# A hybrid decoder block in fp32: small transfers spread between weight loads, and the S5 rotation tables as a task of their own

## The chip, the cores and the metric

The kernel runs on one core of one Trainium2 chip. The core has TensorE (PE: matrix products), VectorE (DVE), ScalarE (ACT), GpSimd (POOL) and SyncE (SP), which here only starts DMA transfers. Each engine works through its own queue of instructions in order and waits on semaphores for the others. The metric is the device time of one execution in microseconds; lower is better. Times of a kernel are the median of several runs.

## The reference

One layer of a decoder block over 256 tokens of width 2048, all in float32:

```python
xn = rms_norm(x, norm_mix_g)
u_s5, u_lru, q, k, v, gate_logits = split(xn @ w_in)      # 2048 -> 1024 + 1024 + 3*1024 + 3*2048
g_s5, g_lru, g_attn = split(sigmoid(gate_logits + b_gate))
merged = (g_s5 * (s5(u_s5) @ w_br_s5) + g_lru * (rglru(u_lru) @ w_br_lru)
          + g_attn * (stick_breaking_attention(q, k, v) @ w_br_attn))
h = x + merged @ w_out
hdn = relu(rms_norm(h, norm_mlp_g) @ w_up)                # 2048 -> 8192
return rms_norm(h + (hdn * hdn) @ w_down, final_norm_g)
```

`s5` is a complex diagonal state space layer (64 groups of 16 channels with 64 states each: `h = lam_bar * h + b_bar u`, then the real part of `c h`, a skip, GELU, and a sigmoid gate over `w_glu`). `rglru` is a convolution of width 4, two block-diagonal gates, and a real linear recurrence. The attention has 8 heads of 128; a weight is `exp(log_sigmoid(z) + sum of log_sigmoid(-z) over the later keys)`, causal.

## The kernel before, in words

**The weight stream.** All dense weights pass in one fixed order as 520 units of 512 KB (128 partitions x 2 x 512 columns): 0 to 15 the LRU inputs, 16 to 31 the S5 inputs, then for each of four column blocks of the LRU gate 8 units of `w_in` and 4 of `w_br_lru` (32 to 79), 80 to 127 six chunks of k, q and v, then four times 8 + 4 for the attention gate and `w_br_attn` (128 to 175), 176 to 231 the S5 gates, `w_glu` and `w_br_s5`, 232 to 263 `w_out`, and then `w_up` and `w_down`. A unit is loaded by SP (L130, `raw`, three buffers), and since a product in float32 is made of three products of shorter floats, ACT rounds it to `hi` (L146) and DVE subtracts to get `lo` (L147; three buffers each). PE uses a unit in `chunk` (24 matmuls of 256 columns, L225 to L227) or in `chunk_tok` and `pair_tok` (12 matmuls of 512 columns, L241 to L243 and L276 to L278): hi times hi, lo times hi, hi times lo. The PE groups in the profile are called `mm_`, `mt_` and `mp_` for these three.

**Side work.** Everything else is written as Python generators with `yield` between their steps. `later(gens, rate)` makes a task of them, and after each unit `pump()` advances each task by `rate` steps. What a step issues is placed behind that unit's matmuls and the casts made with it. There is no other planner: the number of yields and the rate set the order of the side work against the weight units on each engine; the compiler's scheduler then settles the rows of each queue.

**The side work that the change touches.** `s5_params` makes the S5 parameters. `lru_half` runs half of the LRU: convolution, gates, tanh, exp, square root, scan. `s5_scan` (rate 1.27) runs 8 blocks: for each, four `ps_v` products (their inputs are spread over partitions by 12 small transfers, `stk`, L627, on SP), a copy (L653), a rotation by a table of cosine and sine, four scans, and a rotation back. The table of a block, `tc` and `ts` of 128x1024, comes from `s5_tables`: a sum on DVE (L604), a rounding on ACT (L606) and DVE (L607), Abs (L609) and two Sins on ACT (L610, L611). `gates` brings a piece of the gate bias over SP (`gb`, L739), runs a gate chunk on PE, and then a multiply and add on DVE (L744) and a Sigmoid on ACT (L745). `attention` runs each head's logits `z`, `s = ln(1 + exp(-|z|))` (L789 to L792, with DVE at L793 and L794), a cumulative sum on PE (`ps_c`, L800 to L802) and an Exp (L805). ACT's functions come in sets, and a function of another set needs an `ACT_TABLE_LOAD` ahead of it on ACT's queue. The second norm's sum over the columns is one small matmul group `ps_n` (L977). The residual `x_res` (2 MB) is loaded at L918 and the final norm's weights `gfb` (1 MB) at L989, both started from ACT's queue.

Of the kernel before, what the change touches and what calls it, by code (L numbers as in the profile page):

```python
# [9 lines left out]
F32 = mybir.dt.float32  # L10
# [36 lines left out]
def hybrid_block(ctx: ExitStack, tc: tile.TileContext, io, out):  # L47
# [62 lines left out]
    st = {"load": 0, "split": 0, "use": 0}  # L110
# [121 lines left out]
    def chunk_tok(name, c, k, xs, hold=0, done=None):  # L232
# [12 lines left out]
        for g in range(ng - hold):  # L245
# [5 lines left out]
            anchor["pe"] = mm.ins  # L251
            pump()
# [158 lines left out]

    def s5_params():
# [55 lines left out]
        for k, (p, q, op) in enumerate(((cb_, ib_, ALU.add), (ib_, cb_, ALU.subtract))):  # L468
# [5 lines left out]
            for h in range(2):  # L474
                r_ = slice(64 * h, 64 * h + 64)
                nc.vector.tensor_tensor(ce[r_, k, :, h, :], u[r_, 0], u[r_, 1], op)
                yield

# [43 lines left out]

    def lru_half(c, us):
        parts = []
        for m in range(2):
            if m == 0:
                t = [lp.tile([P, 2, L], F32, tag=n_, name=f"lru_{n_}{c}") for n_ in ("xc", "r", "i", "th")]
            else:
                w4 = [pp.tile([P, 2, 2, L], F32, tag=n_, name=f"lru_{n_}{c}", bufs=2) for n_ in ("tc", "ts")]
                t = [w_[:, k] for w_ in w4 for k in range(2)]  # L530
# [8 lines left out]
        yield  # L539
# [12 lines left out]
        yield  # L552
# [42 lines left out]
    def s5_tables(b):  # L595
        c = pp.tile([P, NT, 16, 16], F32, tag="tc", name=f"tc{b}", bufs=2)
        s = pp.tile([P, NT, 16, 16], F32, tag="ts", name=f"ts{b}", bufs=2)
        q = slice(b * NT, (b + 1) * NT)
        sh = [P, NT, 16, 16]
        f = "p n a b -> p (n a b)"  # L600
        cf, sf = c.rearrange(f), s.rearrange(f)

        def gen():
            nc.vector.tensor_tensor(c, fhi[:, q, :].unsqueeze(3).broadcast_to(sh), flo[:, q, :].unsqueeze(2).broadcast_to(sh), ALU.add)  # L604
            yield
            nc.scalar.activation(sf, cf, AF.Identity, bias=magic)  # L606
            nc.vector.scalar_tensor_tensor(sf, sf, -MAGIC, cf, ALU.add, ALU.subtract)  # L607
            yield
            nc.scalar.activation(cf, sf, AF.Abs)  # L609
            nc.scalar.activation(sf, sf, AF.Sin, scale=-TURN)  # L610
            nc.scalar.activation(cf, cf, AF.Sin, scale=-TURN, bias=half_pi)  # L611
            yield
        f = "p n a b -> p n (a b)"
        return (c.rearrange(f), s.rearrange(f)), gen()

# [15 lines left out]
    def s5_scan():  # L631
# [3 lines left out]
        tabs, more = s5_tables(0)  # L635
        yield from more
# [5 lines left out]
        for _ in range(4):  # L642
            yield
        tt = nc.vector.tensor_tensor
        for b in range(WT):
            c, s = tabs
# [9 lines left out]
            more = iter(())  # L656
            if b + 1 < WT:
                s5_split(b + 1)
                tabs, more = s5_tables(b + 1)
                yield  # L660
# [11 lines left out]
            next(more, None)  # L672
# [482 lines left out]
```

## Time and profile before

| | |
|---|---|
| median of three runs | 1522.82 us (1517.03, 1522.82, 1524.22) |
| the profiled execution | 1518.29 us, its span 1516.4 us |
| busy in the span | PE 1489.1 us (98%), DVE 1176.4 (78%), ACT 783.9 (52%), POOL 35.1 (2%) |
| mean granted clock of PE | 0.995 |
| HBM traffic | 282.71 MB read, 188 GB/s over the span |
| weight units on SP's queue | 512 KB each, about 4.2 us from issue to landing |

Busy time counts an instruction from its start to its modelled end. A row of a timeline has the start, the duration, the engine, the line, the operation and its tiles, and in brackets how long the engine had been idle before it and what released it. A row of the waits says which engine waited at which line for which engine's line: the total, how many times, and the longest. `SPq` and `ACTq` are transfers started from those engines' queues.

### The profile page before, as it was taken

The numbers are of one execution on the slowest core, as the hardware profiler recorded it, in microseconds if no ns is written. First come the engines' busy times: TensorE is split into PE (matmuls) and PEld (weight loads), VectorE is DVE, ScalarE is ACT, GpSimd is POOL, SyncE is SP. The second block draws the span as 40 slices with busy tenths as digits, with TensorE's granted clock in tenths as the row PEclk, the third lists the DMA queues.
The fourth block names the chain that finished last, engine by engine and source line by source line (L and its number), as shares of the span: only waits on it lengthen the run. The fifth ranks groups of instructions, "written<-read, shape, count | busy, mean of one in ns | idle before, by whom it ended". The sixth has DMA issues, their size and how long they took to land.

```text
span 1516.4 us, 19895 instructions
## 1 busy us (share of the span) xinstructions
PE 1489.1 (98%) x7518; PEld 1260.0 (83%) x7518; DVE 1176.4 (78%) x1468; ACT 783.9 (52%) x920; POOL 35.1 (2%) x60
## 2 busy tenths in 40 slices
PE   9998999999999999999999999999999999999997
PEld 9996888989887878988787888888888888888886
DVE  6767988897988989689699797568855787558965
ACT  6767556565765564544355444344433444344443
POOL 1400000000000000000000000000000000000011
PEclk9999999999999999999999999999999999999999
DMA  9445766655555756565756556666666666666664
GB/s 291 152 151 180 214 205 201 187 182 170 176 174 179 211 185 210 185 204 187 268 179 189 185 181 207 194 191 198 193 195 192 192 190 198 191 194 192 193 196 152
DMA packets 88914, 292.41 MB, mean 193 GB/s; under 512 B 12786, under 2 KB 17010, under 8 KB 88562
## 3 DMA queue, kind: packets, MB, share of 16 engines
q1 hardware_dynamic: 88386, 287.93, 61.0%
q10 hardware_dynamic: 432, 3.21, 0.6%
q8 instruction: 59, 0.97, 0.3%
q14 instruction: 37, 0.30, 0.1%
HBM read 282.71 MB, written 2.10 MB: 188 GB/s over the span
## 4 chain that ended last, share of the span: by engine, by line
PE 81%; DVE 11%; issue 4%; ACT 2%; DMA 2%; SPq 0%; DVEq 0%; ACTq 0%
PE mt_w_up L242 6%; PE mt_w_up L243 6%; PE mt_w_up L241 6%; PE mt_w_in L242 5%; PE mt_w_in L243 5%; PE mt_w_in L241 5%; DVE lo L147 4%; PE mt_w_down L242 4%; PE mt_w_down L241 4%; PE mt_w_down L243 4%; PE mp_w_down L277 4%; PE mp_w_down L278 4%; PE mp_w_down L276 4%; PE mm_w_in L227 4%; PE mm_w_in L225 4%
## 5 line engine op out<-in xcount | busy, mean ns | idle before, releaser
L146 ACT CAST hi<-raw 128x1024 fp32r<-128x1024 f32 (+1 forms) x521 | 546.4, 1051 | 629.6 <-PE mt_w_up L243 131.6
L147 DVE TENSOR_TENSOR lo<-raw,hi 128x1024 fp32r<-128x1024 f32 (+1 forms) x521 | 638.2, 1226 | 289.4 <-ACT hi L146 285.6
L242 PE MATMUL mt_w_in<-lo,xhi 128*128 128x512 f32 x448 | 176.0, 393 | 3.5 <-DVE lo L147 3.4
L241 PE MATMUL mt_w_in<-hi,xhi 128*128 128x512 f32 x448 | 175.0, 395 | 0.2 <-ACT hi L146 0.2
L243 PE MATMUL mt_w_in<-hi,xlo 128*128 128x512 f32 x448 | 175.1, 391 | 0.0
L241 PE MATMUL mt_w_up<-hi,hhi 128*128 128x512 f32 x448 | 174.3, 389 | 0.0
L242 PE MATMUL mt_w_up<-lo,hhi 128*128 128x512 f32 x448 | 174.3, 389 | 0.0
L243 PE MATMUL mt_w_up<-hi,hlo 128*128 128x512 f32 x448 | 174.3, 389 | 0.0
L227 PE MATMUL mm_w_in<-xhi,lo 128*128 128x256 f32 x512 | 145.4, 286 | 4.7 <-DVE lo L147 4.7
L225 PE MATMUL mm_w_in<-xhi,hi 128*128 128x256 f32 x512 | 146.5, 286 | 0.4 <-ACT hi L146 0.4
L226 PE MATMUL mm_w_in<-xlo,hi 128*128 128x256 f32 x512 | 145.7, 285 | 0.0
L729 DVE STREAM_TRANSPOSE reluT<-relu 32x256 f32<-32x256 f32 x256 | 111.5, 435 | 4.2
L242 PEld LDWEIGHTS mt_w_in<-lo,xhi 128*128 128x128 f32 x448 | 84.6, 189 | 23.2 <-DVE lo L147 6.7
L227 PEld LDWEIGHTS mm_w_in<-xhi,lo 128*128 128x128 f32 x512 | 98.7, 194 | 5.7 <-DVE lo L147 5.7
L242 PE MATMUL mt_w_down<-lo,hd_hi 128*128 128x512 f32 (+1 forms) x272 | 102.5, 377 | 0.0
L241 PE MATMUL mt_w_down<-hi,hd_hi 128*128 128x512 f32 (+1 forms) x272 | 102.4, 377 | 0.0
L243 PE MATMUL mt_w_down<-hi,hd_lo 128*128 128x512 f32 (+1 forms) x272 | 102.4, 376 | 0.0
L277 PE MATMUL mp_w_down<-lo,hd_hi 128*128 128x512 f32 x256 | 99.8, 390 | 0.1
L225 PEld LDWEIGHTS mm_w_in<-xhi,hi 128*128 128x128 f32 x512 | 99.1, 194 | 0.9 <-ACT hi L146 0.7
L276 PE MATMUL mp_w_down<-hi,hd_hi 128*128 128x512 f32 x256 | 99.6, 389 | 0.0
L278 PE MATMUL mp_w_down<-hi,hd_lo 128*128 128x512 f32 x256 | 99.6, 389 | 0.0
L226 PEld LDWEIGHTS mm_w_in<-xlo,hi 128*128 128x128 f32 x512 | 99.2, 194 | 0.1
(299 smaller groups left out, 2356.1 us busy)
## 6 DMA issues: line engine op xcount, KB each, us to landing
raw<-in_w_in SPq DMA_DIRECT2D x175, 512.0 KB, 4.2
raw<-in_w_up SPq DMA_DIRECT2D x128, 512.0 KB, 4.3
raw<-in_w_down SPq DMA_DIRECT2D x128, 512.0 KB, 4.2
raw<-in_w_out SPq DMA_DIRECT2D x32, 512.0 KB, 4.2
raw<-in_w_br_lru SPq DMA_DIRECT2D x16, 512.0 KB, 4.2
raw<-in_w_br_attn SPq DMA_DIRECT2D x16, 512.0 KB, 3.9
raw<-in_w_br_s SPq DMA_DIRECT2D x16, 512.0 KB, 4.2
stk<-ux SPq DMA_DIRECT2D x96, 64.0 KB, 4.0
```

The source lines that it names most:

```text
L146: anchor["act"] = nc.scalar.copy(h[:, k, :], r[:, k, :]).ins
L147: anchor["dve"] = nc.vector.tensor_tensor(l_[:, k, :], r[:, k, :], h[:, k, :].bitcast(F32), ALU.subtract).ins
L225: nc.tensor.matmul(o, wh[:, kk, s], xh, start=first and ct % 2 == 0, stop=False, skip_group_check=True)
L226: nc.tensor.matmul(o, wh[:, kk, s], xl, start=False, stop=False, skip_group_check=True)
L227: mm = nc.tensor.matmul(o, wl[:, kk, s], xh, start=False, stop=last and ct % 2 == 1, skip_group_check=True)
L241: nc.tensor.matmul(banks[j], xh[:, s], wh[:, a:b], start=kt == 0, stop=False)
L242: nc.tensor.matmul(banks[j], xh[:, s], wl[:, a:b], start=False, stop=False)
L243: return nc.tensor.matmul(banks[j], xl[:, s], wh[:, a:b], start=False, stop=kt == ng * UK - 1)
L276: nc.tensor.matmul(o, xh[:, s], wh[:, kk, :], start=kt == 0, stop=False)
L277: nc.tensor.matmul(o, xh[:, s], wl[:, kk, :], start=False, stop=False)
L278: mm = nc.tensor.matmul(o, xl[:, s], wh[:, kk, :], start=False, stop=kt == ng * UK - 1)
L729: nc.vector.transpose(d_[32 * a:32 * a + 32, :, :, 32 * b:32 * b + 32], s_[32 * b:32 * b + 32, :, :, 32 * a:32 * a + 32])
```

## The change

It does seven things. (1) `s5_tables` becomes a task of its own that starts six steps after it is made, with more yields; before its Sins it pauses while a gate chunk is open and fewer than three of its units are left (`st["gate"]`, `st["left"]`). The first table is made at the end of `s5_params`. (2) `lru_half` gives up one yield and puts one into a loop; its second tiles are allocated once. (3) The first block's `stk` transfers get a yield after each `s5_stack`. (4) The gate bias is loaded three steps later. (5) The residual is loaded in four pieces from SP's queue, one in four steps. (6) The final norm's weights are loaded from SP's queue, at a later place of the program. (7) The second norm gets three more yields ahead of `ps_n`.

```diff
--- before.py
+++ after.py
@@ -107,7 +107,7 @@
             "w_out": D, "w_up": D, "w_down": DFF}
 
...
-    st = {"load": 0, "split": 0, "use": 0}
+    st = {"load": 0, "split": 0, "use": 0, "gate": False, "left": 0}
 
     def pieces(i):
         return [slice(k, k + 1) for k in range(UK)] if i == 0 else [slice(0, UK)]
@@ -249,6 +249,7 @@
                 for j in range(len(cols)):
                     mm = mms(j, g * UK + kk, wh[:, kk, :], wl[:, kk, :])
             anchor["pe"] = mm.ins
+            st["left"] = ng - 1 - g
             pump()
         held = [next_unit() for _ in range(hold)]
         for j in range(len(cols)):
@@ -409,6 +410,34 @@
         nc.sync.dma_start(bco, io["s5_b"])
         yield
 
+    def s5_tables(b):
...
+        def gen():
+            nc.vector.tensor_tensor(c, fhi[:, q, :].unsqueeze(3).broadcast_to(sh), flo[:, q, :].unsqueeze(2).broadcast_to(sh), ALU.add)
+            yield
+            yield
+            nc.scalar.activation(sf, cf, AF.Identity, bias=magic)
+            nc.vector.scalar_tensor_tensor(sf, sf, -MAGIC, cf, ALU.add, ALU.subtract)
+            yield
+            yield
+            nc.scalar.activation(cf, sf, AF.Abs)
+            yield
+            while st["gate"] and st["left"] < 3:
+                yield
+            nc.scalar.activation(sf, sf, AF.Sin, scale=-TURN)
+            nc.scalar.activation(cf, cf, AF.Sin, scale=-TURN, bias=half_pi)
+            yield
+        f = "p n a b -> p n (a b)"
+        return (c.rearrange(f), s.rearrange(f)), gen()
+
+    tab0 = []
+
     def s5_params():
         lr, li, dt, a, b, n, w, den, sh, ch, ea, em, xr, xi, cr, ci = (prm[:, k, :] for k in range(16))
         g = nc.gpsimd
@@ -475,6 +504,9 @@
                 r_ = slice(64 * h, 64 * h + 64)
                 nc.vector.tensor_tensor(ce[r_, k, :, h, :], u[r_, 0], u[r_, 1], op)
                 yield
+        tabs, more = s5_tables(0)
+        tab0.append(tabs)
+        yield from more
 
     nq = later([norm1()], 1)
     later([s5_load()], 1)
@@ -520,14 +552,15 @@
     ylru_hi = ypool.tile([P, WT, L], F32R, tag="yhi", name="ylru_hi")
     ylru_lo = ypool.tile([P, WT, L], F32R, tag="ylo", name="ylru_lo")
 
+    lw = [pp.tile([P, 2, 2, L], F32, tag=n_, name=f"lru_{n_}", bufs=2) for n_ in ("tc", "ts")]
+
     def lru_half(c, us):
         parts = []
         for m in range(2):
             if m == 0:
                 t = [lp.tile([P, 2, L], F32, tag=n_, name=f"lru_{n_}{c}") for n_ in ("xc", "r", "i", "th")]
             else:
-                w4 = [pp.tile([P, 2, 2, L], F32, tag=n_, name=f"lru_{n_}{c}", bufs=2) for n_ in ("tc", "ts")]
-                t = [w_[:, k] for w_ in w4 for k in range(2)]
+                t = [w_[:, k] for w_ in lw for k in range(2)]
             cts = [(j, slice(4 * c + 2 * m + j, 4 * c + 2 * m + j + 1)) for j in range(2)]
             parts.append((us[m], cts, *t))
         for u, cts, xc, r, i_, th in parts:
@@ -536,7 +569,6 @@
                 for s in range(1, 4):
                     nc.vector.scalar_tensor_tensor(xc[:, j, s:], u[:, j, :L - s], cw[:, 3 - s, k], xc[:, j, s:], ALU.mult, ALU.add)
                 yield
-        yield
         for u, cts, xc, r, i_, th in parts:
             for j, k in cts:
                 ps = pss.tile([P, CH], F32, tag="ps", name=f"ps_l{c}_{k.start}")
@@ -549,7 +581,7 @@
             for j, k in cts:
                 nc.scalar.activation(th[:, j, :], r[:, j, :], AF.Tanh, scale=sp4[:, k])
             nc.vector.tensor_tensor(i_, i_, xc, ALU.mult)
-        yield
+            yield
         for u, cts, xc, r, i_, th in parts:
             for j, k in cts:
                 nc.scalar.activation(r[:, j, :], r[:, j, :], AF.Exp, scale=nsp8[:, k])
@@ -591,27 +623,6 @@
 
 
     S5_RATE = 1.27
-
...
     def s5_split(ct):
         bx = [ux[:, 2 + i, :].rearrange("p (r g s) -> p r g s", r=2, g=2) for i in range(2)]
@@ -632,17 +643,18 @@
         v = ypool.tile([P, 2, NT, L], F32, tag="yhi", name="s5_v")
         t12 = ypool.tile([P, 2, NT, L], F32, tag="ylo", name="s5_t")
         vr, vi, t1, t2 = v[:, 0], v[:, 1], t12[:, 0], t12[:, 1]
-        tabs, more = s5_tables(0)
-        yield from more
+        tabs = tab0[0]
+        more = None
         s5_split(0)
         yield
         yield
         for t in range(NT):
             s5_stack(t)
-        for _ in range(4):
             yield
         tt = nc.vector.tensor_tensor
         for b in range(WT):
+            if more is not None:
+                finish(more)
             c, s = tabs
             t3 = pp.tile([P, NT, L], F32, tag="t3", name=f"t3_{b}")
             for t in range(NT):
@@ -653,10 +665,10 @@
                 nc.scalar.copy(v[:, :, t, :], v2(ps))
                 if t % 2:
                     yield
-            more = iter(())
             if b + 1 < WT:
                 s5_split(b + 1)
                 tabs, more = s5_tables(b + 1)
+                more = later([chain_of(6, more)], S5_RATE)
                 yield
             tt(t1, vr, c, ALU.mult)
             yield
@@ -669,7 +681,6 @@
             tt(vr, vr, s, ALU.mult)
             yield
             tt(t3, t3, vr, ALU.subtract)
-            next(more, None)
             yield
             for x_ in (t1, t3):
                 for t in range(NT):
@@ -678,11 +689,9 @@
                     if b + 1 < WT and x_ is t1:
                         s5_stack(t)
                     yield
-            next(more, None)
             tt(t2, t1, c, ALU.mult)
             yield
             tt(vr, t3, s, ALU.mult)
-            next(more, None)
             yield
             tt(t2, t2, vr, ALU.subtract)
             yield
@@ -702,6 +711,11 @@
             if b % 2:
                 gq.append(later([gelu(b)], 1.0))
 
+    def chain_of(n, gen):
+        for _ in range(n):
+            yield
+        yield from gen
+
     def tt_scan(o, r, i):
         nc.vector.tensor_tensor_scan(o, r, i, 0.0, ALU.mult, ALU.add)
 
@@ -736,8 +750,17 @@
     def gates(idx, c, alloc):
         gb = tmp.tile([P, CH], F32, tag="gbias", name=f"gb{idx}_{c}", bufs=1)
         o = idx * D + c * CH
-        nc.sync.dma_start(gb, repeat(io["b_gate_row"][:, o:o + CH], P))
+
+        def bias():
+            for _ in range(3):
+                yield
+            nc.sync.dma_start(gb, repeat(io["b_gate_row"][:, o:o + CH], P))
+            yield
+
+        later([bias()], 1.0)
+        st["gate"] = True
         banks = chunk_tok("w_in", GATE0 + 4 * idx + c, D, xs)
+        st["gate"] = False
         gts = []
         for j in range(2):
             g = alloc(c, j).rearrange("p a l -> p (a l)")
@@ -915,7 +938,15 @@
     mlp = ctx.enter_context(tc.tile_pool(name="mlp", bufs=1))
     gp = small("norm_mlp_g")
     x_tok = mlp.tile([P, 2, D], F32, name="xres")
-    nc.scalar.dma_start(x_tok, io["x_res"])
+
+    def x_load():
+        for c in range(4):
+            s = slice(c * CH, (c + 1) * CH)
+            nc.sync.dma_start(x_tok[:, :, s], io["x_res"][:, :, s])
+            for _ in range(4):
+                yield
+
+    later([x_load()], 1.0)
     mf.append(chained(mq, split_tok(3, mlp.tile([P, 4, L], F32, tag="reluT", name="mT3", bufs=2))))
     hT = act.tile([P, KT, L], F32, tag="m16", name="hT")
     hhi = act.tile([P, KT, L], F32R, tag="xhi", name="hhi")
@@ -970,7 +1001,8 @@
             yield
         for n in (2, 1):
             nc.vector.tensor_tensor(hT[:, 0:n, :], hT[:, 0:n, :], hT[:, n:2 * n, :], ALU.add)
-        yield
+        for _ in range(4):
+            yield
         a = hT[:, 0, :]
         ps = pss.tile([P, CH], F32, tag="ps", name="ps_n2")
         for t in range(2):
@@ -986,7 +1018,6 @@
     ho = mlp.tile([P, 2, D], F32, name="ho")
     ssq = mlp.tile([P, 2, 6], F32, name="ssq")
     rf = mlp.tile([P, 2], F32, name="rf")
-    nc.scalar.dma_start(gfb, repeat(io["final_norm_g"], P))
 
     def down_evac(t, s, bank):
         nc.vector.scalar_tensor_tensor(h_tok[:, t, s], bank, rs2[:, t:t + 1], h_tok[:, t, s], ALU.mult, ALU.add)
@@ -1079,6 +1110,8 @@
                         total(t, c)
                     nc.gpsimd.tensor_tensor(ho[:, t, s], h_tok[:, t, s], gfb[:, s], ALU.mult)
 
+        if q == 1:
+            nc.sync.dma_start(gfb, repeat(io["final_norm_g"], P))
         pair_tok("w_down", 0, FQ, hs_, down_done)
         for c in range(2, 4):
             if q == NQ - 1 and c == 3:
```

What the order becomes on SP around the first gate chunk. The rows are transfers in the order in which SP starts them; the first `raw` of `in_w_br_lru` is unit 40. Before:

```order
L130 DMA raw_1484<-in_w_in 128x1024
L627 DMA stk<-ux 32x2x256
L130 DMA raw_1508<-in_w_in 128x1024
L627 DMA stk<-ux 32x512
L627 DMA stk<-ux 32x2x256 x2
L627 DMA stk<-ux 32x512
L627 DMA stk<-ux 32x2x256 x2
L627 DMA stk<-ux 32x512
L627 DMA stk<-ux 32x2x256 x2
L627 DMA stk<-ux 32x512
L627 DMA stk<-ux 32x2x256
L130 DMA raw_1538<-in_w_br_lru 128x1024
```

Now:

```order
L638 DMA stk<-ux 32x512
L638 DMA stk<-ux 32x2x256
L130 DMA raw_1490<-in_w_in 128x1024
L638 DMA stk<-ux 32x512
L638 DMA stk<-ux 32x2x256 x2
L638 DMA stk<-ux 32x512
L638 DMA stk<-ux 32x2x256
L130 DMA raw_1515<-in_w_in 128x1024
L638 DMA stk<-ux 32x2x256
L638 DMA stk<-ux 32x512
L638 DMA stk<-ux 32x2x256
L130 DMA raw_1536<-in_w_br_lru 128x1024
```

The small transfers that stood in one block ahead of unit 40 lie between the loads of the last units of the gate chunk.

On ACT shortly behind a gate chunk. First the second column block of the LRU gate, from the cast of unit 54 on, in the branch chunk behind the gate chunk, before:

```order
L146 CAST hi_1883<-raw_1854 128x1024
L745 ACTIVATE gate_1_0_1873<-gate_1_0_1873 128x512
L745 ACTIVATE gate_1_1_1876<-gate_1_1_1876 128x512
L146 CAST hi_1902<-raw_1881 128x1024
L606 ACTIVATE ts_1660<-tc_1659,magic 128x1024
L146 CAST hi_1923<-raw_1900 128x1024
L609 ACTIVATE tc_1659<-ts_1660 128x1024
```

and now:

```order
L146 CAST hi_1887<-raw_1858 128x1024
L433 ACT_TABLE_LOAD
L433 ACTIVATE ts_1614<-ts_1614 128x1024
L768 ACT_TABLE_LOAD
L768 ACTIVATE gate_1_0_1877<-gate_1_0_1877 128x512
L768 ACTIVATE gate_1_1_1880<-gate_1_1_1880 128x512
L434 ACT_TABLE_LOAD
L434 ACTIVATE tc_1613<-tc_1613,half_pi 128x1024
L146 CAST hi_1908<-raw_1885 128x1024
L146 CAST hi_1927<-raw_1906 128x1024
```

A table's two Sins have come to stand around the gates' Sigmoids, ahead of the cast of unit 55. Then the same place in the attention gate's second column block, from the cast of unit 150 on, before:

```order
L146 CAST hi_4654<-raw_4623 128x1024
L609 ACTIVATE tc_4380<-ts_4381 128x1024
L610 ACT_TABLE_LOAD
L610 ACTIVATE ts_4381<-ts_4381 128x1024
L745 ACT_TABLE_LOAD
L745 ACTIVATE gate_1_0_4644<-gate_1_0_4644 128x512
L745 ACTIVATE gate_1_1_4647<-gate_1_1_4647 128x512
L611 ACT_TABLE_LOAD
L611 ACTIVATE tc_4380<-tc_4380,half_pi 128x1024
L146 CAST hi_4676<-raw_4652 128x1024
L146 CAST hi_4695<-raw_4674 128x1024
```

and now:

```order
L146 CAST hi_4658<-raw_4629 128x1024
L146 CAST hi_4677<-raw_4656 128x1024
L768 ACT_TABLE_LOAD
L768 ACTIVATE gate_1_0_4648<-gate_1_0_4648 128x512
L768 ACTIVATE gate_1_1_4651<-gate_1_1_4651 128x512
L146 CAST hi_4696<-raw_4675 128x1024
L146 CAST hi_4733<-raw_4694 128x1024
```

The table is gone from that place, and the Sigmoids stand behind the cast of unit 151.

On ACT in the second half of the attention, between the casts of units 126 and 129 (`z` and `s` are those of heads 6 and 7, `ts` and `tc` a table). Before:

```order
L146 CAST hi_4044<-raw_4009 128x1024
L789 COPY z_4031<-ps_z_4033 128x384
L790 ACTIVATE s_4032<-z_4031 128x384
L791 ACTIVATE s_4032<-s_4032 128x384
L792 ACTIVATE s_4032<-s_4032 128x384
L146 CAST hi_4088<-raw_4042 128x1024
L789 COPY z_4075<-ps_z_4077 128x384
L790 ACTIVATE s_4076<-z_4075 128x384
L791 ACTIVATE s_4076<-s_4076 128x384
L805 ACTIVATE z_3965<-z_3965 128x384
L792 ACTIVATE s_4076<-s_4076 128x384
L146 CAST hi_4114<-raw_4086 128x1024
```

and now, from head 6's copy on:

```order
L812 COPY z_4041<-ps_z_4043 128x384
L433 ACT_TABLE_LOAD
L433 ACTIVATE ts_3759<-ts_3759 128x1024
L813 ACTIVATE s_4042<-z_4041 128x384
L434 ACTIVATE tc_3758<-tc_3758,half_pi 128x1024
L814 ACT_TABLE_LOAD
L814 ACTIVATE s_4042<-s_4042 128x384
L828 ACTIVATE z_3975<-z_3975 128x384
L815 ACT_TABLE_LOAD
L815 ACTIVATE s_4042<-s_4042 128x384
L812 COPY z_4081<-ps_z_4083 128x384
L146 CAST hi_4094<-raw_4052 128x1024
```

Two Sins of a table now stand among the attention's Abs, Exp and Ln, with loads of function sets between them; a further Exp and Ln of head 7, each with a load ahead, follow behind the casts of units 127 to 129.

More of the change, by code (lines that the diff above doesn't have):

```diff
@@ L410, in s5_load @@
         yield
+    def s5_tables(b):
+        c = pp.tile([P, NT, 16, 16], F32, tag="tc", name=f"tc{b}", bufs=2)
+        s = pp.tile([P, NT, 16, 16], F32, tag="ts", name=f"ts{b}", bufs=2)
+        q = slice(b * NT, (b + 1) * NT)
+        sh = [P, NT, 16, 16]
+        f = "p n a b -> p (n a b)"
+        cf, sf = c.rearrange(f), s.rearrange(f)
+        def gen():
[16 more added lines that the diff above has]
+    tab0 = []
     def s5_params():
@@ L593, in hybrid_block @@
     S5_RATE = 1.27
[L595 to L604, printed above, removed]
-            yield
[L606 to L614, printed above, removed]
     def s5_split(ct):
@@ L972, in norm2 @@
             nc.vector.tensor_tensor(hT[:, 0:n, :], hT[:, 0:n, :], hT[:, n:2 * n, :], ALU.add)
-        yield
+        for _ in range(4):
+            yield
         a = hT[:, 0, :]
```

## The prediction

> **What bounds the kernel now.** I read the busy shares, then what TensorE (PE) waited for, then slices of 40 us, then the timelines around the waits.
>
> ```profile
> span 1516.4 us, 19895 instructions
> PE 1489.1 (98%) x7518; PEld 1260.0 (83%) x7518; DVE 1176.4 (78%) x1468; ACT 783.9 (52%) x920; POOL 35.1 (2%) x60
> ```
> ```profile
> PE mm_w_in L227 <- DVE lo L147: 4.7, 5, 1.9
> PE mt_w_in L242 <- DVE lo L147: 3.4, 5, 1.8
> PE ps_n L977 <- DVE hT L972: 2.3, 1, 2.3
> PE mt_w_br_attn L241 <- ACT hi L146: 2.2, 1, 2.2
> PE mt_w_br_lru L241 <- ACT hi L146: 2.0, 1, 2.0
> PE mp_w_out L277 <- DVE lo L147: 0.8, 1, 0.8
> PE mp_w_out L276 <- ACT hi L146: 0.6, 1, 0.6
> ```
> PE is busy 98% of the span, so a change of side work can give back only what PE waits, plus what a lowered clock costs after a wait. The second fence (total us, times, longest) says where: a weight half (hi from ScalarE, ACT; lo from VectorE, DVE) that comes late because its engine was in side work, and once a norm matmul placed too early. The slices (length, busy us and counts of PE, PEld, DVE, ACT, POOL, then granted clock, DMA share, GB/s) put places to them:
>
> ```profile
> 80.00:120.00 40.00, 37.19 (x262) 35.17 (x261) 28.26 (x42) 28.65 (x42) 0.00 (x0) 0.96 0.46 142
> 120.00:160.00 40.00, 35.89 (x145) 28.26 (x144) 28.39 (x35) 25.05 (x33) 0.00 (x0) 0.91 0.63 197
> 480.00:520.00 40.00, 37.41 (x176) 29.18 (x175) 34.37 (x39) 25.40 (x31) 0.00 (x0) 1.00 0.60 184
> 640.00:680.00 40.00, 40.00 (x178) 33.14 (x177) 32.97 (x45) 17.45 (x18) 0.00 (x0) 1.00 0.65 200
> 720.00:760.00 40.00, 38.59 (x168) 31.07 (x167) 27.83 (x36) 15.52 (x15) 0.00 (x0) 1.00 0.77 264
> 800.00:840.00 40.00, 36.71 (x162) 29.39 (x161) 36.69 (x59) 20.34 (x25) 0.00 (x0) 1.00 0.60 185
> ```
> The slice at 640 is what an undisturbed stretch looks like: 40.00 of 40.00 in 178 matmuls, so a unit of 12 of them takes 2.7. A clock of 0.96 is 0.04 x 40 = 1.6 us lost, one lowering; 0.91 is 3.6 us, two. They follow some waits of about 2 us and not others: none at 480 or 800, where the waits were 2.2 and 2.3. So I price a lowering at 1.7 us and its chance after a wait of 2 us or more at about 0.6 (three of five).
>
> **The change, part by part.** Units count the weight tiles from 0, as in the order of instructions.
>
> *Second LRU half to the first branch (units 25 to 42).* Before:
>
> ```profile
> 91.05 1.22 DVE L147 TENSOR_TENSOR lo<-raw,hi 128x1024 fp32r<-128x1024 f32 x1
> 92.32 0.41 PE L227 MATMUL mm_w_in<-xhi,lo 128*128 128x256 f32 x1 [1.92 <-DVE lo L147]
> 131.71 7.04 SPq L627 DMA_DIRECT2D stk<-ux  x11
> 138.79 1.56 SPq L130 DMA_DIRECT2D raw<-in_w_br_lru  x3
> 135.13 1.28 ACT L745 ACT_TABLE_LOAD   x1
> 141.59 1.31 ACT L745 ACTIVATE gate<-gate 128x512 f32<-128x512 f32 x2 [5.18 <-DVE gate L744]
> 142.81 2.13 ACT L146 CAST hi<-raw 128x1024 fp32r<-128x1024 f32 x2
> ```
> Eleven small stk transfers hold SP's queue for 7.04 us ahead of the first branch weight, and ACT waits 5.18 us for the gate with the cast of that weight behind it: PE stands 2.0 us at unit 40 (mt_w_br_lru). The longest wait of mt_w_in for lo, 1.8, is at unit 36. With smaller ones the slice from 120 lacks 40 - 35.89 = 4.1 us, and 3.6 to the clock: 7.7. Now the stk transfers lie between weights, and the cast of unit 40 stands ahead of the gates; since a gate operation of DVE now stands ahead of lo 40, I leave 1.5 of the 2.0 there. Gain 7.7 - 1.5 = 6.2. Against it, the first table moves here. DVE gets the table's sum, 1.1 to 1.2 like every operation on 1024 columns, ahead of lo 26, and nothing covers it: lo 26 starts straight behind other work and PE already waits 1.92 for it: +1.1. ACT gets two Sins (1.07 and 1.15 in the next fence) and one load more (1.28), 3.5 in all, ahead of the casts of units 31 and 32. A cast may start when the unit three before it is done, which leaves it 2 x 2.7 less its own 1.05, a lead of 4.3; of this the LRU's operations in the same place take most, so 0.9 of waiting at 31 and 0.7 at lo 32. Sum -6.2 + 1.1 + 0.9 + 0.7 = -3.5; carrying each engine's new order by hand through the same durations gives -4.7. **I take -4** (-6 if unit 26 absorbs the sum, -2 if a new wait lowers the clock).
>
> *Gate chunk ends.* Before, at the last one of attention:
>
> ```profile
> 476.76 1.05 ACT L609 ACTIVATE tc<-ts 128x1024 f32<-128x1024 f32 x1
> 477.83 1.28 ACT L610 ACT_TABLE_LOAD   x1
> 479.13 1.07 ACT L610 ACTIVATE ts<-ts 128x1024 f32<-128x1024 f32 x1
> 480.20 1.28 ACT L745 ACT_TABLE_LOAD   x1
> 481.49 1.16 ACT L745 ACTIVATE gate<-gate 128x512 f32<-128x512 f32 x2
> 482.65 1.28 ACT L611 ACT_TABLE_LOAD   x1
> 483.95 1.15 ACT L611 ACTIVATE tc<-tc,half_pi 128x1024 f32<-128x1024 f32 x1
> 485.00 2.93 ACT L146 CAST hi<-raw 128x1024 fp32r<-128x1024 f32 x3
> ```
> The gates fall between the two Sins, so three loads stand in 485.00 - 476.76 = 8.2 us of ACT work ahead of the cast of unit 151; PE waits 2.2 and its slice lacks 2.6. In the new order only one load and the gates are left there: 1.28 + 1.16 = 2.4, behind the cast and less than a unit's 2.7. **-2.8** (-3.5 to -2.2). But the same row of three loads, without the Abs, now stands ahead of the cast of unit 55, the place of unit 151 in the second LRU gate, where before were the gates alone. It is 1.05 shorter, so the wait is 2.2 - 1.05 = 1.1, and some 0.4 at a following unit: **+1.5** (0.5 to 3.8, with a lowering). The pause that the diff adds looks at chunks whose gate is still open; here the task goes on just after.
>
> *Attention, second half.* Before, with s and z of 128x384:
>
> ```profile
> 404.79 0.48 ACT L789 COPY z<-ps_z 128x384 f32<-128x384 f32 x1 [0.49 <-PE ps_z L788]
> 405.30 0.53 ACT L790 ACTIVATE s<-z 128x384 f32<-128x384 f32 x1
> 407.57 0.51 ACT L792 ACTIVATE s<-s 128x384 f32<-128x384 f32 x1
> 407.99 1.03 ACT L146 CAST hi<-raw 128x1024 fp32r<-128x1024 f32 x1
> 408.71 0.42 DVE L794 TENSOR_TENSOR s<-s,keep 128x256 f32<-128x256 f32 x1
> L800 PE MATMUL ps_c<-s,tri x8: 377/379/381, 403.1 to 414.8; 128*128 128x256 f32 x8
> ```
> The last head's s is ready at 409.1 and PE uses it at 414.8: 5.7 us of cover. No load stands between these operations, since one set preloaded at L807 holds Exp and Ln. Now a table's Sins stand among them; behind these Exp and Ln are each given a load of their own. From the copy of head 6 to the last Ln of head 7, ACT gets five loads (6.4), two Sins (2.2) and two casts that were behind (2.1): 10.7 us. Less the 5.7 it is 5.0 of waiting, some 1.3 at unit 127 (its cast is behind the Sins) and 3.7 at the last ps_c; DVE's extra 1.22 ahead of keep is inside what is uncertain. **+5** (2 if heads run earlier, 7 if DVE adds its own), and with 0.6 x 1.7 = 1.0 for a lowering **+6**.
>
> A change of set is priced here by its row, 1.28: the Abs ahead of the load at 477.83 had ended at 477.81, and the Sin started 0.02 behind the load. [...]
>
> *w_out.* Before, the residual x (2 MB, ACT's queue) stands against the weights:
>
> ```profile
> 719.80 0.33 ACTq L918 DMA_DIRECT2D xres<-in_x_res  x1
> 729.08 1.05 ACT L146 CAST hi<-raw 128x1024 fp32r<-128x1024 f32 x1 [6.57 <-DMA raw<-in_w_out]
> 730.38 0.54 ACTq L989 DMA_DIRECT2D gfb<-in_final_norm_g  x1
> xres<-in_x_res ACTq DMA_DIRECT2D x1, 2048.0 KB, 8.6
> ```
> Its 8.6 us make a weight late and PE loses 0.6 + 0.8 = 1.4, the lack of slice 720. In four pieces on SP's queue, three or four weights from first to last, that goes. The 1 MB of gfb now stands on that queue ahead of one weight: by the 2 MB row half of 8.6, 4.3 us, against a cast's lead of about 4 behind it: 0 to 0.8. **-1.2** (-1.6 to 0).
>
> *Second norm.* ps_n goes four steps later, behind more units' matmuls, so that hT is ready: the 2.3 of the third wait goes, and nothing else waits for rs2 before the end of w_down's first group. **-2.3** (-2.5 to -1.5). The gate bias, three steps later, has a gate chunk of 8 units to land: 0.
>
> Sum: -4 - 2.8 + 1.5 + 6 - 1.2 - 2.3 = **-2.8 us**.
>
> **The rivals.** (a) *The table in attention is hidden*: if head 6 and 7 start earlier, since DVE and PE have less ahead of them, the 10.7 us meet 5.7 plus the idle ACT time of the stretch (0.49 and what lies between 408 and 411). Then attention costs 0 to 2: -2.8 - 5 = **-7.8**. For it: ACT is 52% busy. Against: the casts stand in the same queue, in that order.
> (b) *The other side: table switching by one engine.* Place: ACT between units 126 and 130. If head 7's chain runs into the casts of 128 and 129, these hold back their raw buffers and the next weights start late, so the wait goes on: +9 with a sure lowering of 1.7 in place of +6, and unit 55 with one, +3.2 in place of +1.5. Sum -2.8 + 4.7 + 1.7 = **+3.6**. It decides once the lead of casts after 128 falls to zero; by hand about 1.8 us of it is left.
> (c) *The waits only move*: the first table's parts at units 26, 31 and 32 each lower the clock, 3.4, and unit 40 stays at 2: the first part is 0 and the sum **+1**.
> [...]
>
> **How the numbers follow.** Chances: my sum 0.45, (a) 0.25, (b) 0.15, (c) 0.11, (d) 0.04. The profiled execution took 1518.29, its span 1516.4 and 1.9 around it. The median of the three runs shown is 1522.82, between 1517.03 and 1524.22, so the profiled one stands low among them. The sum gives 1515.5 from the profiled execution and 1520.0 from the median; nothing here says which a further run is like, and I take **1517**. Range: (a) from the profiled execution, 1510.5, less 1.5 for a lowering that doesn't come, 1509; (b) from the median 1526.4, of which half is left out: 1524. About 0.5%, 7.6 us, is what a measurement of this kernel can tell from no change. Faster by more means below 1515.2: most of (a) and a third of my sum, 0.38. Slower by more means above 1530.4: parts of (b) and (d), and what I have not seen, 0.08. Within: 0.54.
>
> **What would show it.** Right: at 120 to 160 a clock near 1.00 and PE above 37.5; no wait of mt_w_br_lru over 1.6; at 480 PE near 40; no wait of ps_n; two more ACT_TABLE_LOADs in all; a wait of ps_c for s, keep (L794 before) or of unit 127 together near 5 us around 405 to 420; about 1 us of hi at the second w_br_lru chunk. Wrong: no ps_c wait (then (a)); casts behind unit 130 late as well, with more than 7 us lost from 400 to 440 (then (b)); a lowered clock at 80 to 120 of 0.91 (then (c)); gaps over 1 us ahead of loads (then (d)); or x pieces that make weights of w_out late by more than before.

## The result

The changed kernel takes **1513.62 us** (median of four runs, 1511.02 to 1514.55) against 1521.38 for the kernel before: the ratio is **0.9949**, 95% interval 0.9928 to 0.9970. A later set of six runs gave 1512.52 and 0.9944 (0.9928 to 0.9961). So it is faster by about half a per cent. The forecast, 1517 with 1509 to 1524, was 3.4 us too high, and its sum, -2.8, well under half of the -7.8 between the medians. Of the chances, "within 0.5%" had 0.54 and "faster by more" 0.38; at -0.51% with that interval the two can't be told apart.

The page of the changed kernel begins so:

```profile
span 1509.3 us, 19913 instructions
PE 1483.1 (98%) x7518; PEld 1256.1 (83%) x7518; DVE 1175.3 (78%) x1468; ACT 783.8 (52%) x922; POOL 36.1 (2%) x60
```
The span fell by 7.1 us. What PE waited for (total, times, longest):

```profile
PE mm_w_in L227 <- DVE lo L147: 5.5, 5, 1.9
PE ps_c L823 <- DVE s L817: 3.4, 1, 3.4
PE mt_w_in L242 <- DVE lo L147: 2.4, 4, 1.4
PE mm_w_in L225 <- ACT hi L146: 1.4, 2, 0.8
PE mt_w_br_lru L241 <- ACT hi L146: 1.3, 1, 1.3
PE mt_w_br_lru L242 <- DVE lo L147: 0.8, 1, 0.8
```
The waits of ps_n, of `mt_w_br_attn` and of w_out are gone. Three are new: ps_c 3.4, and of `mt_w_br_lru` 1.3 for hi, which is now unit 55 and no longer unit 40, and 0.8 for lo at unit 40. In the rows of mm_w_in and mt_w_in, unit 31 has 0.8 and 0.6, which it had not before, and unit 32 went from 0.7 to 1.4. The 40 us slices, with the same columns as before (PE busy is the second number, the clock the third from the end):

```profile
80.00:120.00 40.00, 35.15 (x259) 33.11 (x258) 28.63 (x42) 30.88 (x46) 0.00 (x0) 1.00 0.44 134
120.00:160.00 40.00, 38.45 (x171) 30.95 (x170) 32.98 (x41) 22.07 (x28) 0.00 (x0) 1.00 0.72 210
160.00:200.00 40.00, 38.49 (x182) 30.41 (x181) 33.93 (x38) 25.54 (x30) 0.00 (x0) 1.00 0.67 208
400.00:440.00 40.00, 36.56 (x187) 29.52 (x186) 28.27 (x41) 29.25 (x42) 0.00 (x0) 1.00 0.44 137
480.00:520.00 40.00, 40.00 (x191) 32.11 (x190) 38.81 (x46) 24.27 (x31) 0.00 (x0) 1.00 0.74 213
720.00:760.00 40.00, 40.00 (x178) 33.12 (x177) 29.97 (x42) 15.95 (x17) 0.00 (x0) 1.00 0.84 281
800.00:840.00 40.00, 39.02 (x172) 31.57 (x171) 34.57 (x53) 21.18 (x27) 0.00 (x0) 1.00 0.59 192
```
In the kernel before, the slices at 160 and 400 lacked nothing:

```profile
160.00:200.00 40.00, 40.00 (x191) 32.55 (x190) 38.39 (x41) 22.59 (x23) 0.00 (x0) 1.00 0.65 203
400.00:440.00 40.00, 40.00 (x206) 33.17 (x205) 34.49 (x47) 27.06 (x39) 0.00 (x0) 1.00 0.53 169
```
So waits went, wholly or for the most part, from the slices at 120, 480, 720 and 800, and others came at 80, 160 and 400. The clock is 1.00 in all of them; before it was 0.96 and 0.91 in the first two. At the prediction's price of 1.7 us the three lowerings of the kernel before would be 5.1 of the 7.1 us, and the waits only 2.0; the next section shows that this price is too high. The first question for the experiments was whether the lowerings belong to the program.

### The profile page after: what moved, and what is told of

It reads as the page before. It is cut to its first block, busy times and chain, and to the rows that moved or that the text cites. A ratio compares the mean times of both kernels' runs of the same rounds, so it can differ in the third digit from the quotient of the medians.

```text
span 1509.3 us, 19913 instructions
## 1 busy us (share of the span) xinstructions
PE 1483.1 (98%) x7518; PEld 1256.1 (83%) x7518; DVE 1175.3 (78%) x1468; ACT 783.8 (52%) x922; POOL 36.1 (2%) x60
## 4 chain that ended last, share of the span: by engine, by line
PE 77%; DVE 12%; ACT 4%; issue 4%; DMA 2%; POOL 0%; SPq 0%; DVEq 0%; ACTq 0%
PE mt_w_up L243 6%; PE mt_w_up L242 6%; PE mt_w_up L241 6%; PE mt_w_in L242 5%; PE mt_w_in L241 5%; PE mt_w_in L243 5%; DVE lo L147 4%; PE mt_w_down L242 4%; PE mt_w_down L241 4%; PE mt_w_down L243 4%; PE mp_w_down L278 4%; PE mp_w_down L279 4%; PE mp_w_down L277 4%; PE mm_w_in L227 3%; PE mm_w_in L226 3%
## 5 line engine op out<-in xcount | busy, mean ns | idle before, releaser
L241 PEld LDWEIGHTS mt_w_in<-hi,xhi 128*128 128x128 f32 x448 | 84.1, 188 | 18.1 <-issue 0.8
```

Of the source, the lines that this page charges most:

```text
L241: nc.tensor.matmul(banks[j], xh[:, s], wh[:, a:b], start=kt == 0, stop=False)
```

## Where a lowered clock comes from

A lowering is a stretch at a granted clock of 0.50 in place of 1.00. In the first profile of the kernel before there are three, each 3.413 us long, at 92.55, 130.10 and 143.75 us, 11 and 4 times 3.413 apart; in the run with added waits below, stretches at 0.50 start at 416.66, 1014.00 and 1075.44 us, 175 and 18 times 3.413 apart. So I speak of a beat of 3.413 us. Its place against the kernel's start differs from run to run: in three profiles with the same program up to there, a beat starts at 411.25, 411.48 or 413.25 us. (The end of every run is left out here and below: PE stands still there, and the clock was 0.50 from 1512.50 us on in the kernel before and from 1503.51 us on in the changed one, whose beats are counted back from there.) Here are four beats of the kernel before, around the wait at unit 26, and then three of the changed one, around that of ps_c:

```profile
85.73:89.14 3.41, 3.24 (x27) 3.04 (x26) 3.41 (x8) 3.33 (x6) 0.00 (x0) 1.00 0.40 114
89.14:92.55 3.41, 1.49 (x13) 1.29 (x12) 3.41 (x7) 1.31 (x2) 0.00 (x0) 1.00 0.20 77
92.55:95.97 3.42, 3.42 (x18) 3.42 (x18) 3.42 (x7) 0.00 (x0) 0.00 (x0) 0.50 0.56 176
95.97:99.38 3.41, 3.41 (x29) 3.41 (x29) 2.16 (x3) 1.15 (x2) 0.00 (x0) 1.00 0.82 259
```
```profile
411.25:414.66 3.41, 1.70 (x8) 1.06 (x6) 1.19 (x4) 3.36 (x5) 0.00 (x0) 1.00 0.72 243
414.66:418.08 3.42, 1.78 (x10) 1.62 (x11) 3.42 (x7) 3.35 (x5) 0.00 (x0) 1.00 0.04 16
418.08:421.49 3.41, 3.41 (x17) 2.80 (x16) 3.41 (x6) 1.88 (x3) 0.00 (x0) 1.00 0.50 154
```
At unit 26 PE was idle for 1.92 of one beat, and the next ran at half clock: 18 matmuls where 29 fit. The wait of ps_c was longer, 3.35 us, but the end of a beat halved it: 1.71 idle and 1.64, and no lowering. To test that, both kernels ran again unaltered, and the changed one also with waits added.

**The changed kernel once more.**

> The changed kernel once more, unaltered. Theory (the waits belong to the program, the lowerings to where a wait falls on the beat of 3.413 us): the same waits as in its first profile within 0.1 us each (ps_c 3.4, unit 26 1.9, unit 32 1.4, unit 55 1.3), but lowerings that differ: over phases the 3.4 us wait should lower the clock 19 times in 20 and the 1.9 about every second time, so 1 or 2 lowerings here against none in the first profile, and a span of 1509.3 + 1.7 per lowering. Rival (a lowering follows from the program): none again, span within 0.5 of 1509.3.

Measured: span 1510.3, one lowering, 0.7 less than 1509.3 + 1.7. Of the waits named, unit 55 had 1.4 (1.3 before) and the others were the same within 0.1 us; some at units 13, 14 and 37, all under 1.6, differ by up to 1. The wait of ps_c, 3.4 again, now fell into one beat:

```profile
411.48:414.89 3.41, 0.07 (x1) 0.00 (x0) 2.12 (x4) 3.37 (x5) 0.00 (x0) 1.00 0.41 141
414.89:418.30 3.41, 3.35 (x10) 2.91 (x11) 3.41 (x6) 2.30 (x4) 0.00 (x0) 0.50 0.21 62
```
**The kernel before once more.**

> The kernel before once more, unaltered. Theory: the waits of its first profile again (1.6, 1.9, 1.8, 2.0, 2.2, 2.3) within 0.1 us, lowerings at other places than units 26, 36 and 40 alone, two to four in number, and a span that is 1511.3 + 1.7 per lowering. Rival: lowerings at the same three places, span 1516.4 within 0.5.

Measured: span 1520.9, clock 0.991, and lowerings over six beats, behind the waits at units 36, 40 (two beats), 151, in w_out and at the second norm; none at 26, whose wait of 1.93 was there again. Unit 40 waited 0.3 us longer than in the first profile, the others named the same within 0.1. 1520.9 - 6 x 1.7 = 1510.7, close to the 1511.3 expected; the number of lowerings was larger than "two to four". That the two agree does not make 1511.3 the time without lowerings, as is shown below.

**Waits added.** In the changed kernel (the table `PAUSE` itself is left out here):

```diff
-            anchor["act"] = nc.scalar.copy(h[:, k, :], r[:, k, :]).ins
+            if i in PAUSE:                      # 24 units, nine apart
+                for _ in range(PAUSE[i][0]):    # 0 or 1
+                    nc.scalar.copy(h[:, k, :], r[:, k, :])
+            anchor["act"] = nc.scalar.copy(h[:, k, :], r[:, k, :]).ins
+            if i in PAUSE:
+                for _ in range(PAUSE[i][1]):    # 3 to 6
+                    nc.vector.tensor_tensor(l_[:, k, :], r[:, k, :], h[:, k, :].bitcast(F32), ALU.subtract)
```


> The changed kernel with the subtraction for lo (in some cases also the cast for hi) done 4 to 7 times over at 24 units of the MLP, nine units apart, so that PE waits there by 0.5 to 5 us; the result is the same. Theory (the lowerings seen start at a fixed beat of 3.413 us and follow a beat in which PE was idle for more than about 1.75 us): every beat with 1.9 us idle or more is followed by a beat at half clock, none with 1.6 or less is; a wait of 2 to 3.4 us that lies across the end of a beat has none. Rival (the length of the wait alone decides): all waits over some length lower the clock, wherever they lie.

Measured: 1633.9 us. Two neighbouring beats with one wait of 3.70 us across them, and the one behind:

```profile
1068.61:1072.02 3.41, 1.79 (x8) 1.13 (x7) 3.41 (x4) 1.05 (x1) 0.00 (x0) 1.00 0.33 85
1072.02:1075.44 3.42, 1.34 (x6) 1.13 (x7) 3.28 (x6) 0.00 (x0) 0.00 (x0) 1.00 0.34 95
1075.44:1078.85 3.41, 3.41 (x10) 2.67 (x9) 2.60 (x6) 1.04 (x1) 0.00 (x0) 0.50 0.74 251
```
Behind the 1.63 us idle of the first the clock stayed at 1.00, behind the 2.07 of the second it was 0.50. Over all twelve profiles, without the last three beats of each, of the beats at full clock all 22 with 1.93 us idle or more were followed by half clock, 11 of 19 between 1.64 and 1.92, 2 of 47 between 1.0 and 1.63, and none of 5132 below. So both bounds that I had set were a little too strict: one beat of this run with 1.91 us idle was followed by full clock, and the two low ones, in other profiles, had 1.54 and 1.47 (the latter with PE partly in the one-column products of ps_n). In these profiles the lowering goes with the idle time of the beat ahead, without a sharp bound: from 1.64 to 1.92 us, about half of the 3.41, both occurred. The rival falls: the 3.4 us wait of ps_c lowered the clock in two of the three profiles that have it (in the second profile of the changed kernel and in this run, not in the first), and a wait of 3.70 us counted by its parts.

An estimate from this beat, with 1.75 us out of those 1.64 to 1.92 as the bound: for phases that fall at random, a wait of g (at least 1.75) leaves 1.75 or more in one beat with probability (3.41 + g - 3.5) / 3.41: 0.5 for 1.8, 0.66 for 2.35, 0.95 for 3.35. Summed over the waits above 1.75 the estimate is 2.9 for the kernel before (5 waits) and 1.5 for the changed one (2 waits), 1.4 lowerings or, at 1.7 each, 2.4 us apart. With the 2.0 of waits that makes -4.4. The medians of the two sets of runs say -7.8 and -9.2, and the near ends of their intervals are -4.6 and -5.9, so this sum falls short. The kernel before showed 3 and 6 lowered beats, more than the sum gives it, among them one behind a wait that comes in two pieces (w_out), which the sum leaves out.

The price is wrong too. Profiles that have the same program in a stretch, with and without a lowering there, give it by the starts of the units' first matmuls. From unit 25 to 34 the kernel before took 34.2 and 34.1 us with the lowering (its first profile, and the run of the late parts below, which is the same program up to there) and 33.3 without (its second): 0.9. From unit 148 to 160, behind unit 151, it took 39.3 with it (second profile) and 38.6 without (first): 0.7. From unit 264 to 290, at the second norm, 77.0 with it and 75.4 without: 1.6. From unit 126 to 131, at ps_c, the changed kernel took 21.9 with it and 20.3 without: 1.6. At the first of these places a wait behind the lowering was shorter for it: unit 32 waits 0.7 with the lowering and 1.1 without.

So the split into 5.1 and 2.0 does not hold. The granted clocks of the single runs say the same: two runs of the kernel before had a mean clock of 0.998, which leaves room for at most one lowering, and spans of 1514.8 and 1514.9; the changed kernel had 1509.3 at 0.998. These are 5.5 us apart with at most one lowered beat on one side and none on the other. Over all runs whose clock was recorded, 27 and 10, the mean spans are 1518.6 and 1511.2, 7.3 apart. By this estimate most of the gain is there without lowered clocks, and some 2 us come from having fewer of them; how far a lowering changes the waits behind it was measured at these four places alone.

## Experiments on the parts

**The attention's table, and the gate's.** Two guards in the changed kernel, `attn` set between an attention half's first logits and its last cumulative sum, `since` the units after a gate chunk, `force` for a table that is needed at once (where the three are set is left out):

```diff
-            while st["gate"] and st["left"] < 3:
+            while not st["force"] and (st["attn"] or (st["left"] < 3 if st["gate"] else st["since"] < 3)):
                 yield
```


> The changed kernel with a table's Sins held back while an attention half is between its first logits and its last cumulative sum, and for three units behind a gate chunk. Theory (the waits are the table's, at those two places, and nothing else needs the table there): the wait of ps_c for s (3.4 us) and that of unit 55 for its cast (1.3, with 0.4 behind it) go, nothing takes their place, and the span falls by 3.9 + 1.8 = 5.7 us, to about 1503.6 against 1509.3 of the changed kernel without a lowered clock. Rival (the waits only move): the table comes so late that its block's rotation waits for it, DVE's lo casts behind it, and PE waits as much within ten units: span within 2 us of 1509.

Measured: **1504.07 us**, ratio to the kernel before 0.9897 (0.9882 to 0.9912); span 1502.5 with one lowering at unit 26, which the changed kernel's first profile had not. The waits of ps_c and at unit 55 are gone and nothing took their place: 1509.3 - 1502.5 = 6.8 in spite of the lowering is more than the 5.7 expected without one. By the starts of the matmuls the two places gave 4.2 and 2.4, and smaller waits went as well: at units 13 and 14 (1.2 less), 31 (0.4), 37 (0.5) and 46 (0.2), some of which differ from run to run. The rival is out.

**The loads alone.** The same Sins in attention, but behind them one load of the set that has Exp and Ln:

```diff
             nc.scalar.activation(cf, cf, AF.Sin, scale=-TURN, bias=half_pi)
+            if st["attn"]:
+                tc.keep_in_program_order(nc.scalar.preload_act_table_set("natural_log_exp_and_others"))
```


> The changed kernel with one load of the set that holds both Exp and Ln placed behind a table's Sins while attention runs, so that the Exps and Lns behind it need no load each; the Sins stay. Theory (the price in attention is mostly the five loads, 6.4 us, on the way to head 7's sum): two of these loads fewer ahead of the last ps_c, whose wait falls from 3.4 by 2.6 to about 0.8. Rival (the price is the two Sins and the casts standing ahead): the wait stays above 2.5.

In the changed kernel head 7's way on ACT was this:

```profile
406.72 0.46 ACT L812 COPY z<-ps_z 128x384 f32<-128x384 f32 x1
407.07 1.05 ACT L146 CAST hi<-raw 128x1024 fp32r<-128x1024 f32 x1
408.03 0.52 ACT L813 ACTIVATE s<-z 128x384 f32<-128x384 f32 x1
408.45 1.04 ACT L146 CAST hi<-raw 128x1024 fp32r<-128x1024 f32 x1
409.50 1.28 ACT L814 ACT_TABLE_LOAD   x1
410.79 0.53 ACT L814 ACTIVATE s<-s 128x384 f32<-128x384 f32 x1
411.23 1.03 ACT L146 CAST hi<-raw 128x1024 fp32r<-128x1024 f32 x1
412.27 1.28 ACT L815 ACT_TABLE_LOAD   x1
413.57 0.52 ACT L815 ACTIVATE s<-s 128x384 f32<-128x384 f32 x1
```
and with the one load:

```profile
406.34 0.46 ACT L814 COPY z<-ps_z 128x384 f32<-128x384 f32 x1
406.70 1.05 ACT L146 CAST hi<-raw 128x1024 fp32r<-128x1024 f32 x1
407.65 0.52 ACT L815 ACTIVATE s<-z 128x384 f32<-128x384 f32 x1
408.07 1.04 ACT L146 CAST hi<-raw 128x1024 fp32r<-128x1024 f32 x1
409.01 0.53 ACT L816 ACTIVATE s<-s 128x384 f32<-128x384 f32 x1
409.43 1.04 ACT L146 CAST hi<-raw 128x1024 fp32r<-128x1024 f32 x1
410.38 0.53 ACT L817 ACTIVATE s<-s 128x384 f32<-128x384 f32 x1
```
Measured: 1507.25 us, one run. From head 6's copy to head 7's Ln three loads stand instead of five; Ln ends at 410.91 instead of 414.09, and no wait of ps_c is left, where 0.8 was expected. With the Sins still in place, units 120 to 136 take 1.2 us more than in the kernel before, against 4.3 in the changed one. So most of the price was the two loads, and the rival is out. Each load costs its 1.28 us and 0.01 to 0.02 around it.

**The first stretch.** The kernel before with the small transfers spread, alone, and with the first table moved, alone:

```diff
         for t in range(NT):
             s5_stack(t)
-        for _ in range(4):
             yield
```


> The kernel before with only the spreading of the first block's small transfers. Theory (SP's queue held the weight of unit 40): the wait of mt_w_br_lru at unit 40 (2.0 us) falls under 1.2 while that of unit 36 for lo (1.8) stays, since the first table still stands there. Rival (unit 40 waited for the gate on ACT, not for the weight): the 2.0 stays as it is.

> The kernel before with only the first table made at the end of the S5 parameters instead of in the S5 scan. Theory (the first table's work on ACT and DVE was behind the wait of 1.8 at unit 36): that wait falls under 0.6, those of units 26, 31 and 32 rise by 1 to 3 in all, the small transfers still come in one block. Rival (the block of small transfers holds the weights of units 36 and 40): the waits at 36 and 40 stay at 1.8 and 2.0.

Spreading alone: span 1517.4, with lowerings at four places. The wait of `mt_w_br_lru` is gone altogether, that of unit 36 stays:

```profile
128.19 0.50 PE L242 MATMUL mt_w_in<-lo,xhi 128*128 128x512 f32 x1 [1.91 <-DVE lo L147]
```
The first table alone: span 1518.3, with lowerings at two. Its waits:

```profile
PE mm_w_in L227 <- DVE lo L147: 5.5, 4, 3.1
PE mt_w_in L241 <- ACT hi L146: 4.0, 2, 2.7
PE mt_w_br_lru L241 <- ACT hi L146: 1.2, 1, 1.2
```
Unit 26 waits 3.1 instead of 1.9: the table's sum costs the 1.1 that I had worked out. In the whole change it waits 1.9 again; there the LRU's convolution starts ahead of lo 25, at 84.5 us instead of 87.1, which fits the moved yields, but these weren't run alone. The waits at units 36 and 40 go: 36 as the theory had it, 40 although the small transfers still come in one block, so in these runs either part by itself removes it. Units 26, 31 and 32 together rise by only 0.4, since the 0.7 at unit 32 goes, where 1 to 3 was expected; but 0.8 comes at unit 37, 1.2 at 38 and at 54, 1.3 at 46, and 2.7 in attention, at unit 130, which I had not foreseen. Neither part shows a gain alone: one run each, inside the spans of the kernel before (1514.8 to 1522.6).

**The late parts.** The kernel before with the residual in pieces and the norm's three steps, the final norm's weights left on ACT's queue:

> The kernel before with only the residual in four pieces on SP's queue and the three further steps ahead of ps_n; the final norm's weights stay on ACT's queue. Theory (both gains are independent of the rest): the waits at w_out (0.6 and 0.8) and of ps_n (2.3) go, and from unit 230 to unit 300 PE needs 2.2 + 2.5 = 4.7 us less, as in the changed kernel. Rival: the final norm's weights, which now start about when the first pieces do, make a weight of w_out late by 0.5 or more.

Measured: span 1513.2. From unit 230 to 300 PE needs 3.0 us less, not 4.7. The wait of ps_n goes. That of w_out hardly does: 0.3 and 0.8 are left of 0.6 and 0.8, as the rival had it. The 1 MB now starts with the first piece, and the cast of the weight behind them waits 6.28 us, as before (6.57), against 3.98 in the changed kernel:

```profile
719.43 0.54 ACTq L998 DMA_DIRECT2D gfb<-in_final_norm_g  x1
728.35 1.05 ACT L146 CAST hi<-raw 128x1024 fp32r<-128x1024 f32 x1 [6.28 <-DMA raw<-in_w_out]
```
So it isn't enough to take the residual off ACT's queue; whether taking off the 1 MB alone would do wasn't tried.

**A version that beats both.** Both holds, and the first table a few steps later:

```diff
-        yield from more
+        yield from chain_of(8, more)
```


> As the kernel before it, and the first table is started seven steps later, so that its sum no longer stands ahead of lo 26 and its Sins stand ahead of the cast of unit 36, where ACT was idle 1.7 us waiting for a weight. Theory: unit 26 waits 0.8 instead of 1.9, units 31 and 32 together 1.0 instead of 2.9, up to 1 us comes back at units 35 to 37, so 2 us less than the kernel before it. Rival: DVE and ACT are full in this stretch and the waits move on to units 33 to 40: 0, or 1 us more.

> As the kernel with both holds, and the first table started eight steps later instead of none (or seven), so that its Sins stand behind the cast of unit 37, where ACT was idle twice for over 2 us. Theory: the wait of 2.4 that the seven steps left at unit 35 goes and none over 1.3 us is left between units 25 and 45; span 1497 without a lowered clock, 5.5 us less than with both holds and the table at once. Rival: the first block's rotation now waits for the table, DVE has its operations in a heap, and a wait of 1.5 to 2.5 comes at units 38 to 46: span 1499 to 1501.

With seven steps: 1501.96 us, 0.9884 (0.9864 to 0.9903), 2.1 less than with the holds alone, as expected; unit 26 waits 1.0 and units 31 and 32 no more, but 2.4 comes at unit 35, with a lowering behind it: part of the rival. With eight: **1500.65 us**, 0.9873 (0.9856 to 0.9889). No wait over 1.3 is left between units 25 and 45, as the theory had it, but the span is 1498.7 and not 1497. Its longest waits are

```profile
PE mm_w_in L228 <- DVE lo L147: 3.3, 4, 1.3
PE mt_w_in L243 <- DVE lo L147: 1.1, 3, 0.5
```
and no beat before the end is idle for more than 1.33, so this run has no lowering there; the clocks of the other three, 0.998, leave room for at most one. The four runs lie between 1500.42 and 1500.98, where those of the kernel before, in sets of 4 to 11, lie 4 to 8 us apart.

## Why the prediction was right, and where its sum was not

By the sum's own terms, for the two profiled executions (differences between the starts of the units named, chosen so that the same small matmuls lie in the stretch in both kernels):

| term | from unit to unit | predicted | measured |
|---|---|---|---|
| units 25 to 42 | 25 to 43 | -4 | -5.5 |
| unit 55 | 54 to 110 | +1.5 | +1.7 |
| unit 151 | 148 to 160 | -2.8 | -3.3 |
| attention | 120 to 136 | +5, with lowering +6 | +4.3 |
| w_out | 230 to 264 | -1.2 | -2.3 |
| second norm | 264 to 300 | -2.3 | -2.6 |
| elsewhere | | 0 | +0.6 |
| sum | | -2.8 | -7.1 |

Every term came at its place and with its sign: which waits go and which come was worked out rightly. The signs named came too: at 120 a clock of 1.00 and 38.45 of PE, 40.00 at 480, no wait of ps_n, 35 table loads for 33, 1.3 of hi at the second w_br_lru; only the waits in attention were 3.5 and not near 5. The sizes:

- *Units 25 to 42.* The waits there went down by only 0.7 in all (6.9 to 6.2); in my -4 stood 3.6 of clock and 0.4 of waits. The other 4.8 go with the three lowered beats. I took two lowerings out, and the third, at unit 26, went too, by where its wait fell on the beat: that is luck of this pair, since a wait of 1.9 stands there still and lowered the clock in two of the variants above. The sum's +1.1 at unit 26 didn't come, as said above; +0.9 and +0.7 at units 31 and 32 came as 0.8, 0.6 and another 0.7.
- *Attention.* From head 6's copy to the end of head 7's Ln ACT took 414.09 - 398.44 = 15.7 us against 408.08 - 400.82 = 7.3: 8.4 more and not 10.7, because the stretch before had 1.5 us of idle ACT time and the operations overlap by 0.1 each. Less the cover of 5.7 this is 2.7; the DVE operation ahead of keep, which I had called uncertain, adds its 1.1. The wait at unit 127 was 0.1, not 1.3. The 1.0 for a lowering was 0 in this profile, and 1.6 in the two others that have this wait; with it attention comes to the +6 of the sum, by errors that cancel.
- *w_out.* A slice's missing busy time (1.4) is less than the loss, because a matmul behind a wait has a longer row (0.50 where others have 0.39); the starts give 2.3. The 1 MB on SP's queue, for which I left up to 0.8, was not a cost: with it left on ACT's queue, 2.0 of the 2.3 stay lost.
- *Lowerings.* "0.6 after a wait of 2 us" is near the 0.5 to 0.66 of the estimate above. The 1.7 is too much (0.7 to 1.6 above). And the sum counted the lowerings that the one profile of the kernel before happened to have, three, where others have up to six.

The 3.4 us come from several things. From the profiled execution the sum gives 1515.5 against 1511.02 measured, 4.5 too high; the choice of 1517 adds 1.5; and the changed kernel's median lies 2.6 above its profiled run, which had no lowering and was the fastest of the four. That the forecast came within 3.4 is in part luck: from the median before, 1521.38, the sum gives 1518.6, 5.0 too high.

Rival (a) had the time, 1510.5 from the profiled execution, but not the reason: attention was not hidden. (b) and (c) did not occur: the casts after unit 130 were in time, and the clock at 80 to 120 stayed at 1.00. (d), a load dearer than its row, is shown by no run: a load took its 1.28 us, and the gap ahead of it is 0.02 at most.

## What to carry to other kernels

A task that switches ACT's function set should not run among operations of another set: here each load took 1.28 us, and with the Sins held back from attention the 3.4 us wait of ps_c was gone. Where it must, try one explicit load of the set that those operations use: here three loads in place of five brought the end of head 7's Ln from 414.09 to 410.91 us. Where PE is nearly always busy (98% here), count each wait near 2 us with its chance of a lowered clock (11 of 19 beats with 1.64 to 1.92 us idle, all 22 with 1.93 or more), on both sides of the sum, and take the price from two profiles of the same program rather than from the clock alone. In the version whose beats were idle for at most 1.33 us, none was lowered in the profile, and its four runs lay within 0.6 us, where those of the kernel before lie 4 to 8 apart. Don't split a difference by one pair of profiles when the runs on record show their clocks. Small transfers, and large ones on another queue, are to be looked at together with the weights that they meet: here PE stood 2.0 us at unit 40 behind the first, and 0.6 and 0.8 in w_out behind the second.

## What was not expected of the hardware

One and the same program had 3 beats at a clock of 0.50 in one profile and 6 in another (the kernel before), or 0 and 1 (the changed one), by where its waits fell on a beat of 3.413 us, and this goes with most of the spread between runs: the runs of the kernel before span 1514.8 and 1514.9 us at a mean clock of 0.998, and 1520.9 to 1522.6 at 0.991. Its times went from 1516.5 to 1524.5, and those of the kernel whose waits stay below 1.4 from 1500.4 to 1501.0. A lowered beat cost less than half its length, 1.7 us: 0.7 to 1.6 at the four places measured.
